# A fourth weight quarter split ahead of two combinations, with a query spill and small constants emitted later

## The chip, the cores and the metric

The kernel runs on one core of one Trainium2 chip. The metric is the device time of one launch in microseconds (us). Below, PE is the matrix engine (TensorE), DVE is VectorE, ACT is ScalarE, POOL is GpSimd and SP is SyncE, whose queue starts nearly all transfers (DMAs) here. Each engine has its own queue of instructions; they meet through semaphores. A time with two decimals such as 46.18 is a place in the profiled execution, counted from the start of its span.

## What is computed

One layer of a hybrid decoder runs on 1024 prompt tokens and 8 sample tokens that share the weights. First comes a large projection, then three branches (a gated linear recurrence, windowed attention, attention into 256 memory tokens), a gated merge, and a feed-forward block.

```python
z = x @ w_in
xr, yr, q, k, v, xq, g = jnp.split(z, SPLIT_IDX, axis=-1)
xc, conv_new = causal_conv(xr, conv_buf, conv_w, conv_b)
hs, h_new = rg_lru(xc, h0, lru_wa, lru_ba, lru_wx, lru_bx, lru_lambda)
a_out = hs * jax.nn.gelu(yr, approximate=True)
...
c_out = mem_attn(xq.reshape(B, T, N_XHEADS, XHEAD_DIM), mem_k, mem_v)
gates = jax.nn.sigmoid(g.reshape(B, T, N_BRANCH, D_MODEL) + b_gates)
merged = sum(gates[:, :, n] * (br @ w_branch[n]) for n, br in enumerate((a_out, s_out, c_out)))
h = layer_norm(ALPHA * x + merged @ w_out, ln1_g, ln1_b)
gt, up = jnp.split(h @ w_gate_up, 2, axis=-1)
h = layer_norm(ALPHA * h + (jax.nn.silu(gt) * up) @ w_down, ln2_g, ln2_b)
```

The change lies in the first 70 us or so, where `x @ w_in` begins.

## The kernel before

**Products of float32 numbers.** Every operand of a product is split into a high part (a cast on ACT, line 71) and a low part (a subtraction on DVE, line 72). A product is three matmuls: high by high, high by low, low by high. In the profile the parts of activations are `th` and `tl`, those of weights `u_0h` and `u_0l` and so on.

**The projection.** The output columns are cut into 30 units of two row tiles each (`UNITS`). The first unit, the first query tiles of the memory attention (`xq`), is done by `begin` with plain products while the activations come in by quarters `x`. From the second unit on the product of a 2 x 2 block matrix takes seven products of blocks in place of eight. For these, sums of weight quarters and of activation quarters are formed: `begin` makes the seven activation combinations `ts` once (`change` adds or subtracts quarters of `x` on DVE, line 204, and `keep` splits the result, for each of two halves `p` of the tokens), and `fast_quarter` makes a weight combination `i` of a unit: for `i` 1, 2, 4 and 5 an addition `us` on DVE (line 263), then the split. So `u_3l` is the low part of the weights of the fourth product (`i` = 3), whose weights are a plain quarter. `fast_step` runs product `i` of a unit for both halves, 12 matmuls each (lines 279 to 281, into `ub`, `uc` or `ud`), and copies or adds the result.

**The order.** `project` walks over `todo`, all pairs of unit and product, and asks for each weight combination three products ahead of its use. The first three of the second unit are asked for from within `begin`. A scheduler then orders each engine's instructions by its own plan, in which code that is written earlier is mostly preferred; after that each engine takes them strictly in that order.

**What stands around the change.** At the end of `begin`, `finish.done` takes the first unit's result (`za`, `zb`): for `xq` it copies the sample tokens' queries to `qdc`, and `spill` scales and splits both tiles (`hi_xq` on ACT, line 368; `za` and `zb` in place on DVE, line 369) and writes them to DRAM, to be read by the memory attention long after. It also queues the job `dec_mem`: the sample tokens' queries are turned (`drt`, line 770), copied (`drow_c`, line 771), written to DRAM and loaded again to all partitions (`dcq`, lines 772 and 783), then multiplied with cached keys (`dck`) on DVE, `dcj`, line 789. `lru_consts` computes constants of the recurrence and of the gates, mostly on 8 columns: some 26 DVE instructions and one on ACT (lines 657 to 677). `pump`, called after each product, emits a piece of the queued jobs.

Of the kernel before, what the change touches and what calls it, by code (L numbers as in the profile page):

```python
# [53 lines left out]
class Builder:  # L54
# [100 lines left out]
    def begin(self, rows, finish, load_next, next_quarter):  # L155


        nc, io, h = self.nc, self.io, D // 2
        pair = lambda name: tuple(self.tp.tile([P, 4, QS], F32R, tag="t", name=f"t{e}{name}", bufs=28) for e in "hl")
        x, hl, ts, w, ps = {}, {}, [[None] * 7, [None] * 7], [[None] * 2, [None] * 2], {}  # L160
        cols = lambda th, p: slice(HT * th + QN * p, HT * th + QN * (p + 1))

        def weight(j, e):
            raw = self.half_raw(io["win"][rows[j]][:, e * h:(e + 1) * h], h, f"ur0_{j}{e}")
            if e == 0:
                w[j] = [None, None, pair(f"w{j}")]
            flat = [a.rearrange("p k n -> p (k n)")[:, e * h:(e + 1) * h] for a in w[j][2]]
            w[j][e] = flat
            return lambda: self.split(*flat, raw)

        def keep(name, src, sign=1.0):
            tiles = pair(name)
            hi, lo = (a[:, :, :QN] for a in tiles)
            src = src.rearrange("p (k n) -> p k n", k=4)
            if sign < 0:
                self.split_scaled(hi, lo, src, sign)
            else:
                self.split(hi, lo, src)
            return tiles

        def fetch(kh, th, p):
            x[kh, th, p] = self.x_quarter(kh, th, p)

        def block(kh, th, p):
            hl[kh, th, p] = keep(f"{kh}{th}{p}", x[kh, th, p])

        def quarter(th, p, z):
            tags = ("mm", "t")
            for kh in range(2):
                xh, xl = (a[:, :, :QN] for a in hl[kh, th, p])  # L190
                for j in range(2):
                    if kh == 0:
                        ps[j] = self.bank(tags[j], f"u0{th}{p}{j}")[:, :QN]
                    wh, wl = w[j][kh]
                    for k in range(4):
                        c, first, last = slice(k * P, (k + 1) * P), kh + k == 0, kh == 1 and k == 3
                        nc.tensor.matmul(ps[j], wh[:, c], xh[:, k, :], start=first, stop=False)
                        nc.tensor.matmul(ps[j], wh[:, c], xl[:, k, :], start=False, stop=False)
                        self.last_mm = nc.tensor.matmul(ps[j], wl[:, c], xh[:, k, :], start=False, stop=last).ins
            for j in range(2):  # L200
                nc.scalar.copy(z[j][:, cols(th, p)], ps[j])

        def change(op, p, to, a, b):
            nc.vector.tensor_tensor(x[(*to, p)], x[(*a, p)], x[(*b, p)], op)
            return x[(*to, p)]

        s00 = weight(0, 0)
        fetch(0, 0, 0)
        s10, s01 = weight(1, 0), weight(0, 1)
        fetch(1, 0, 0)  # L210
        s11 = weight(1, 1)
        for th, p in ((0, 1), (1, 0), (1, 1)):
            fetch(0, th, p)
            fetch(1, th, p)
        z = self.zt("za0"), self.zt("zb0")
        s00()
        block(0, 0, 0)
        s10()
        s01()
        block(1, 0, 0)  # L220
        s11()
        quarter(0, 0, z)
        for th, p in ((0, 1), (1, 0), (1, 1)):
            block(0, th, p)
            block(1, th, p)
            quarter(th, p, z)
            if (th, p) == (1, 0):
                load_next()
                next_quarter(0)
        for p in range(2):  # L230
            ts[p][0], ts[p][3], ts[p][5] = hl[0, 0, p], hl[1, 0, p], hl[1, 1, p]
            change(ALU.subtract, p, (1, 1), (1, 1), (0, 1))
            ts[p][1] = keep(f"1_{p}", change(ALU.subtract, p, (0, 1), (0, 0), (0, 1)))
        next_quarter(1)
        for p in range(2):
            ts[p][2] = keep(f"2_{p}", change(ALU.add, p, (0, 0), (1, 1), (0, 0)), -1.0)
        next_quarter(2)
        finish.done(*z)
        for p in range(2):
            ts[p][4] = keep(f"4_{p}", x[1, 1, p])  # L240
        for p in range(2):
            ts[p][6] = keep(f"6_{p}", change(ALU.subtract, p, (1, 0), (0, 0), (1, 0)))
        return ts

    def fast_load(self, u, src0, src1):
        h = D // 2
# [76 lines left out]
    def project(self):  # L323

        nc, io, tc = self.nc, self.io, self.tc
        self.qdc = self.cst.tile([P, KT * NB], F32, name="qdc")
        self.qds = self.cst.tile([P, KT * NB], F32, name="qds")
        self.kd = self.cst.tile([P, 2 * NB], F32, name="kd")
        self.vd = self.cst.tile([NB, 256], F32, name="vd")
        self.lru_setup()  # L330
        self.side, self.pumped = (deque(), deque()), 0
        n = len(UNITS)
        finish = [Finish(self, kind, j) for kind, j in UNITS]
        st = {}

        def load(u):
            a, b = finish[u].rows
            st[u] = self.fast_load(u, io["win"][a], io["win"][b])
            st[u]["load"]((0, 0), (0, 1), (1, 0), (1, 1))

        ts = self.begin(finish[0].rows, finish[0], lambda: load(1), lambda i: self.fast_quarter(st[1], i))
        with tc.issue_after(self.x_loaded):
            self.load_consts()
            self.load_lru()
        self.lru_consts()
        todo = [(u, i) for u in range(1, n) for i in range(7)]
        ahead = 3
        for k, (u, i) in enumerate(todo):
            if i == 1 and u + 1 < n:
                load(u + 1)  # L350
            if k + ahead < len(todo):
                v, j = todo[k + ahead]
                self.fast_quarter(st[v], j)
            self.fast_step(st[u], i, ts, finish[u])
            self.pump()
            if i == 6:
                del st[u]
        while any(self.side):
            self.pump()
        nc.sync.dma_start(self.scr["c"][:, :, TP:T], self.cdec)  # L360
        self.store_lru()
# [950 lines left out]
```

## Time and profile before

| | |
|---|---|
| median of 3 runs | 2013.3 us (2012.09 to 2013.93) |
| the profiled execution's own time | 2013.24 us |
| its span | 2011.5 us |
| PE's mean granted clock | 0.994 |
| PE idle before its first matmul | 6.0 us |
| PE's longest later waits | 4.6 (`bra`, line 105), 4.1 (`uc`, line 281) us |
| the projection's products end near | 658 us |

How the profile is read: the span runs from the first to the last instruction. In a timeline a row gives the start, the duration, engine, line, operation, `out<-in` by the program's names, shapes and a count; a bracket gives how long the engine stood idle before it and what released it. In a table of stretches a row gives the stretch, its length, then for PE, PE's weight loads, DVE, ACT and POOL the busy time with the number of instructions, then PE's granted clock, the DMA engines' share and GB/s. In the list of waits a row gives who waited for whom, the sum in us, how often, and the longest. A group of the page gives the count, the busy time, the mean ns of one, and the idle time ahead.

### The profile page before, as it was taken

Reading aid. Unit: us, or ns where it says so; the run is one execution under the profiler, and the core shown is the slowest. Engines: PE = TensorE matmul, PEld = TensorE weight load, DVE = VectorE, ACT = ScalarE, POOL = GpSimd, SP = SyncE. Lnnn points to the kernel's source line nnn. Section 1 sums busy time; section 2 is a strip of 40 time slices with the busy share of each in tenths; the row PEclk is TensorE's granted clock in tenths of the full one; section 3 lists DMA queues with packets and bytes.
Section 4 is the critical chain, followed back from the end, with each engine's and each line's share of the span. In section 5 each row is a group of like instructions: output and inputs, shape, how many; then the busy total and the mean of one; then the engine's idle time right before and its main releaser. Section 6 shows DMA issues by size and latency. Waiting matters only on the chain.

```text
span 2011.5 us, 35413 instructions
## 1 busy us (share of the span) xinstructions
PE 1962.2 (98%) x13756; PEld 1929.8 (96%) x13756; DVE 1197.3 (60%) x2558; ACT 878.9 (44%) x1921; POOL 112.4 (6%) x160
## 2 busy tenths in 40 slices
PE   7999999999999999999999999999999999999997
PEld 7999999999999899989999999999999999999996
DVE  8789778878665555498876658423222332232457
ACT  6556555546564555398763334322111221122324
POOL 0001000000000000021110002100000000000001
PEclk9999999999999999999999999999999999999999
DMA  5454454563233865667435320111111111111102
GB/s 220 151 174 171 165 190 137 176 197 125 76 142 107 294 217 188 160 187 218 121 87 167 124 87 22 63 63 58 48 43 42 53 49 47 53 43 43 57 28 85
DMA packets 140441, 235.44 MB, mean 117 GB/s; under 512 B 17280, under 2 KB 69584, under 8 KB 140240
## 3 DMA queue, kind: packets, MB, share of 16 engines
q1 hardware_dynamic: 140272, 233.17, 35.8%
q8 instruction: 108, 1.77, 0.4%
q14 instruction: 61, 0.50, 0.1%
HBM read 179.95 MB, written 55.23 MB: 117 GB/s over the span
## 4 chain that ended last, share of the span: by engine, by line
PE 70%; ACT 4%; DVE 3%; DMA 3%; issue 1%; SPq 0%; ACTq 0%; POOL 0%; DVEq 0%; POOLq 0%
PE fg L107 4%; PE fg L105 4%; PE fg L106 4%; PE fu L107 4%; PE fu L105 4%; PE fu L106 4%; PE d L105 3%; PE d L107 3%; PE d L106 3%; PE ub L279 2%; PE ub L281 2%; PE ub L280 2%; PE brs L105 2%; PE brs L106 2%; PE brs L107 1%; PE bra L106 1%
## 5 line engine op out<-in xcount | busy, mean ns | idle before, releaser
L105 PE MATMUL fg<-hH,wfg_h 128*128 128x384 f32 (+1 forms) x528 | 169.2, 320 | 5.9 <-ACT wfg_h L71 3.0
L106 PE MATMUL fg<-hL,wfg_h 128*128 128x384 f32 (+1 forms) x528 | 168.4, 319 | 0.4 <-DVE hL L1053 0.4
L107 PE MATMUL fg<-hH,wfg_l 128*128 128x384 f32 (+1 forms) x528 | 168.3, 319 | 0.2
L107 PE MATMUL fu<-hH,wfu_l 128*128 128x384 f32 (+1 forms) x528 | 167.7, 318 | 0.0
L106 PE MATMUL fu<-hL,wfu_h 128*128 128x384 f32 (+1 forms) x528 | 167.6, 317 | 0.0
L105 PE MATMUL fu<-hH,wfu_h 128*128 128x384 f32 (+1 forms) x528 | 167.6, 318 | 0.0
L1071 DVE TENSOR_TENSOR ft<-ft,fu 128x384 f32<-128x384 f32 (+1 forms) x66 | 33.8, 513 | 141.4 <-PE fu L107 141.3
L1069 DVE SCALAR_TENSOR_TENSOR ft<-ft,fg 128x384 f32<-128x384 f32 (+1 forms) x66 | 33.8, 512 | 139.6 <-ACT ft L1068 137.6
L105 PE MATMUL d<-gH,wd_h 128*128 128x384 f32 (+1 forms) x360 | 114.4, 318 | 0.0
L106 PE MATMUL d<-gL,wd_h 128*128 128x384 f32 (+1 forms) x360 | 114.2, 317 | 0.0
L107 PE MATMUL d<-gH,wd_l 128*128 128x384 f32 (+1 forms) x360 | 114.2, 317 | 0.0
L71 ACT CAST gH<-ft 128x384 fp32r<-128x384 f32 (+1 forms) x66 | 31.7, 480 | 183.2 <-DVE ft L1071 183.1
L105 PEld LDWEIGHTS fg<-hH,wfg_h 128*128 128x128 f32 x528 | 99.6, 189 | 7.3 <-ACT wfg_h L71 3.4
L106 PEld LDWEIGHTS fg<-hL,wfg_h 128*128 128x128 f32 x528 | 99.8, 189 | 1.0 <-DVE hL L1053 0.9
L107 PEld LDWEIGHTS fg<-hH,wfg_l 128*128 128x128 f32 x528 | 99.8, 189 | 0.9 <-DVE wfg_l L72 0.9
L107 PEld LDWEIGHTS fu<-hH,wfu_l 128*128 128x128 f32 x528 | 99.2, 188 | 0.0
L105 PEld LDWEIGHTS fu<-hH,wfu_h 128*128 128x128 f32 x528 | 99.2, 188 | 0.0
L106 PEld LDWEIGHTS fu<-hL,wfu_h 128*128 128x128 f32 x528 | 99.2, 188 | 0.0
L1068 ACT ACTIVATE ft<-fg 128x384 f32<-128x384 f32 (+1 forms) x66 | 30.1, 456 | 139.8 <-PE fg L107 139.8
L1095 DVE SCALAR_TENSOR_TENSOR acc<-d,acc 128x384 f32<-128x384 f32 (+1 forms) x48 | 24.8, 516 | 108.4 <-PE d L107 108.4
L565 ACT ACTIVATE bp<-bp,bst 128x257 f32<-128x257 f32 (+1 forms) x128 | 62.8, 493 | 18.1 <-DVE bst L561 18.0
L281 PE MATMUL uc<-th,u_3l 128*128 128x258 f32 x232 | 66.4, 287 | 4.1 <-DVE u_3l L72 4.1
(960 smaller groups left out, 6857.3 us busy)
## 6 DMA issues: line engine op xcount, KB each, us to landing
ur<-win SPq DMA_DIRECT2D x120, 256.0 KB, 2.9
dck<-cmk SPq DMA_DIRECT2D x32, 256.0 KB, 2.9
dcv<-cmvT SPq DMA_DIRECT2D x32, 256.0 KB, 3.5
st<-scr_q SPq DMA_DIRECT2D x32, 256.0 KB, 5.2
scr_g<-za SPq DMA_DIRECT2D x12, 516.0 KB, 3.3
scr_g<-zb SPq DMA_DIRECT2D x12, 516.0 KB, 4.0
x<-xQ SPq DMA_DIRECT2D x8, 516.0 KB, 8.0
scr_a<-ge SPq DMA_DIRECT2D x8, 516.0 KB, 3.0
```

The lines of the kernel that those rows point to most:

```text
L71: ins = self.nc.scalar.copy(hi, src).ins
L105: nc.tensor.matmul(ps, sh, mh, start=i == 0, stop=False)
L106: nc.tensor.matmul(ps, sh, ml, start=False, stop=False)
L107: self.last_mm = nc.tensor.matmul(ps, sl, mh, start=False, stop=closes and i == last).ins
L279: mm(sh[:, w], xh, start=opens and k == 0, stop=False)
L280: mm(sh[:, w], xl, start=False, stop=False)
L281: self.last_mm = mm(sl[:, w], xh, start=False, stop=k == 3).ins
L565: nc.scalar.activation(x, x, AF.Exp, bias=st[:, g:g + 1], scale=-1.0, accum_out=st[:, 4 + g:5 + g])
L1068: nc.scalar.activation(t, pg, AF.Tanh, scale=0.5)
L1069: nc.vector.scalar_tensor_tensor(t, t, 1.0, pg, op0=ALU.add, op1=ALU.mult)
L1071: nc.vector.tensor_mul(t, t, pu)
L1095: nc.vector.scalar_tensor_tensor(a, ps, 0.5, a, op0=ALU.mult, op1=ALU.add)
```

## The change

```diff
@@ begin
         next_quarter(2)
-        finish.done(*z)
+        next_quarter(3)
         for p in range(2):
             ts[p][4] = keep(f"4_{p}", x[1, 1, p])
         for p in range(2):
             ts[p][6] = keep(f"6_{p}", change(ALU.subtract, p, (1, 0), (0, 0), (1, 0)))
-        return ts
+        return ts, z
@@ project
-        ts = self.begin(finish[0].rows, finish[0], lambda: load(1), lambda i: self.fast_quarter(st[1], i))
+        ts, z0 = self.begin(finish[0].rows, finish[0], lambda: load(1), lambda i: self.fast_quarter(st[1], i))
...
-        self.lru_consts()
...
-            if k + ahead < len(todo):
+            if 0 < k < len(todo) - ahead:
                 v, j = todo[k + ahead]
                 self.fast_quarter(st[v], j)
             self.fast_step(st[u], i, ts, finish[u])
+            if k == 2:
+                finish[0].done(*z0)
+            if k == 4:
+                self.lru_consts()
             self.pump()
```

The fourth weight quarter of the second unit is now asked for in `begin`, ahead of the activation combinations of the fifth and seventh products (`ts` 4 and 6); the loop skips it at its first step. The spill of the first unit and its `dec_mem` job come after the third product of the second unit, the constants after its fifth. No instruction is added or removed. Below the changed lines the line numbers are three higher.

On DVE, the place around the old spill, as a piece of the difference (names carry buffer numbers; a line with - is before, with + the change, without either both):

```order
 L78 SCALAR_TENSOR_TENSOR tl_1_425<-x_126,th_1_424 128x4x258
-L369 SCALAR_TENSOR_TENSOR za_138<-za_138,hi_xq_435 128x1024
+L72 TENSOR_TENSOR tl_0_439<-x_132,th_0_438 128x4x258
 L72 TENSOR_TENSOR u_2l<-us_2_428,u_2h 128x512
-L369 SCALAR_TENSOR_TENSOR zb_139<-zb_139,hi_xq_441 128x1024
-L72 TENSOR_TENSOR tl_0_447<-x_132,th_0_446 128x4x258
-L72 TENSOR_TENSOR tl_1_451<-x_136,th_1_450 128x4x258
+L72 TENSOR_TENSOR u_3l<-ur_01_330,u_3h 128x512
+L72 TENSOR_TENSOR tl_1_443<-x_136,th_1_442 128x4x258
 L204 TENSOR_TENSOR x_122<-x_114,x_122 128x1032
 L204 TENSOR_TENSOR x_128<-x_126,x_128 128x1032
```

`u_3l` has moved up to the row behind `u_2l`; before, it stood behind both spill rows, four `tl`, the two L204 and the first constants.

Also on DVE, in the change, the rows from the second unit's last split to the first rows of the third unit (`u2_0l` is the third unit's first low part; `dcq0` the loaded queries, `za1`, `zb1` the second unit's results):

```order
L72 TENSOR_TENSOR u1_6l_597<-ur1_11_334,u1_6h_596 128x512
L792 SCALAR_TENSOR_TENSOR dcj0_0_0_592,dcs0_587<-dck0_0_590,dcq0_0_588 128x256
L306 TENSOR_TENSOR za1_600<-uc1_0_601,p1s1_0_473 128x258
L792 SCALAR_TENSOR_TENSOR dcj0_0_1_594,dcs0_587<-dck0_0_590,dcq0_0_588 128x256
L306 TENSOR_TENSOR za1_600<-uc1_1_615,p1s1_1_488 128x258
L72 TENSOR_TENSOR u2_0l_630<-ur2_00_490,u2_0h_629 128x512
L308 SCALAR_TENSOR_TENSOR zb1_633<-ub1_0_460,p5s1_0_517 128x258
```

Before, the first `dcj` rows stood ahead of the fifth, sixth and seventh low parts of the second unit, among the constants; now they stand behind the last of these and ahead of `u2_0l`.

On SP, the queue of transfers around the spill and the queries, before:

```order
L370 DMA scr_xq<-hi_xq_435 128x1024
L370 DMA scr_xq<-hi_xq_441 128x1024
L371 DMA scr_xq<-za_138 128x1024
L371 DMA scr_xq<-zb_139 128x1024
L772 DMA dcq_538<-drow_c_539 8x256
L783 DMA dcq_0_546<-dcq_538 128x512
```

and in the change:

```order
L373 DMA scr_xq<-hi_xq_569 128x1024
L373 DMA scr_xq<-hi_xq_575 128x1024
L82 DMA ur_10_494<-win 128x512
L82 DMA ur_11_496<-win 128x512
L775 DMA dcq_580<-drow_c_581 8x256
L82 DMA ur_00_816<-win 128x512
L786 DMA dcq_0_588<-dcq_580 128x512
L374 DMA scr_xq<-za_138 128x1024
L374 DMA scr_xq<-zb_139 128x1024
```

Weight loads `ur` of the third and fourth units have moved ahead of the queries' write and load, and the two `z` tiles of the spill go out behind them.

On ACT the casts of `ts` 4 and of `u_3h` stand where `hi_xq` of the second tile stood; that `hi_xq` follows three result copies later, and `drow_c` stands behind the cast of `u_4h`. On PE the two `drt` transposes stand ahead of the fourth product in place of the second, and six matmuls of the third unit's first product stand ahead of the second unit's seventh.

## The prediction

> **What bounds the kernel now.** The page comes first, then the waits of TensorE (PE) in it.
>
> ```profile
> span 2011.5 us, 35413 instructions
> PE 1962.2 (98%) x13756; PEld 1929.8 (96%) x13756; DVE 1197.3 (60%) x2558; ACT 878.9 (44%) x1921; POOL 112.4 (6%) x160
> L281 PE MATMUL uc<-th,u_3l 128*128 128x258 f32 x232 | 66.4, 287 | 4.1 <-DVE u_3l L72 4.1
> ```
>
> PE is busy 98% of the span, so only an idle piece of PE, or a stretch at a lower clock, can give time back. The third row holds such a piece: the product with the fourth weight quarter once waited 4.1 us for `u_3l`. The timeline of PE shows it, in the second unit:
>
> ```profile
> 41.44 0.28 PE L279 MATMUL uc<-th,u_3h 128*128 128x258 f32 x1
> 41.68 0.28 PE L279 MATMUL uc<-th,u_3h 128*128 128x258 f32 x1
> 46.18 0.39 PE L281 MATMUL uc<-th,u_3l 128*128 128x258 f32 x1 [4.11 <-DVE u_3l L72]
> 50.19 0.29 PE L279 MATMUL ub<-th,u_4h 128*128 128x258 f32 x1
> 53.08 0.28 PE L279 MATMUL ud<-th,u_5h 128*128 128x258 f32 x1
> ```
>
> Four matmuls of the product run, then PE stands 4.11 us. Matmuls from 50.19 to 53.08 are one product of 24, 2.89 us, or 0.120 each. The 20 from 46.18 to 50.19 took 4.01 where 20 x 0.120 is 2.41. The table of stretches says why, and what VectorE (DVE) does meanwhile:
>
> ```profile
> 32.50:46.00 13.50, 9.58 (x80) 9.33 (x79) 13.40 (x18) 9.90 (x19) 0.00 (x0) 1.00 0.51 197
> 46.18:49.81 3.63, 3.63 (x18) 3.63 (x18) 3.63 (x16) 1.95 (x4) 0.00 (x0) 0.53 0.37 131
> 58.00:72.00 14.00, 14.00 (x118) 14.00 (x117) 14.00 (x33) 7.50 (x18) 0.00 (x0) 1.00 0.47 160
> ```
>
> After the wait the granted clock is 0.53. So this place costs 4.11 us of waiting and 4.01 - 2.41 = 1.60 us of slow clock, **5.71 us** together. But DVE is busy without a break before it (13.40 of 13.50) and long after it (14.00 of 14.00). The delay of PE is also what lets DVE catch up.
>
> **The fourth quarter.** DVE before, in its timeline:
>
> ```profile
> 34.00 1.22 DVE L78 SCALAR_TENSOR_TENSOR tl<-x,th 128x1032 fp32r<-128x1032 f32 x1
> 35.14 1.21 DVE L369 SCALAR_TENSOR_TENSOR za<-za,hi_xq 128x1024 fp32r<-128x1024 f32 x1
> 36.28 0.68 DVE L72 TENSOR_TENSOR u_2l<-us,u_2h 128x512 fp32r<-128x512 f32 x1
> 36.88 1.21 DVE L369 SCALAR_TENSOR_TENSOR zb<-zb,hi_xq 128x1024 fp32r<-128x1024 f32 x1
> 40.48 2.37 DVE L204 TENSOR_TENSOR x<-x,x 128x1032 f32<-128x1032 f32 x2
> 42.77 0.17 DVE L657 TENSOR_SCALAR nsnk<-vec 128x16 f32<-128x16 f32 x1
> 45.44 0.69 DVE L72 TENSOR_TENSOR u_3l<-ur,u_3h 128x512 fp32r<-128x512 f32 x1
> 46.19 0.42 DVE L789 SCALAR_TENSOR_TENSOR dcj<-dck,dcq 128x256 f32<-128x256 f32 x1
> 46.53 0.20 DVE L665 RECIPROCAL lruc<-lruc 128x8 f32<-128x8 f32 x1
> ```
>
> From start to start: a row over about 1032 columns holds DVE 1.14 us (34.00 to 35.14), one over 512 columns 0.60 (36.28 to 36.88), one over 256 columns 0.34 (46.19 to 46.53). ACT's part, and the queries' rows on SyncE (SP):
>
> ```profile
> 34.26 1.05 ACT L368 ACTIVATE hi_xq<-zb 128x1024 fp32r<-128x1024 f32 x1
> 37.72 0.36 ACT L771 COPY drow_c<-drt_c 8x256 f32<-8x256 f32 x1
> 40.20 0.38 ACT L304 COPY u2s<-ub 128x258 f32<-128x258 f32 x1 [0.63 <-PE ub L281]
> 38.53 0.34 SPq L772 DMA_DIRECT2D dcq<-drow_c  x1
> 41.29 0.82 SPq L783 DMA_DIRECT2D dcq<-dcq  x2
> dcq<-dcq SPq DMA_DIRECT2D x4, 256.0 KB, 3.4
> ```
>
> In the new order of DVE (first piece shown with the change) the first `tl` of the fifth product takes the place of the spill at 35.14. Its cast takes the place of `hi_xq` on ACT, 34.26 to 35.31, so DVE starts it at 35.35 instead. Then 1.14 for it and 0.60 for `u_2l`: `u_3l` starts at 37.09 and ends at 37.78. PE asks for it at 41.68. The wait of 4.11 goes with 3.9 us to spare, and with it the slow clock: **-5.71 us**.
>
> **What is late next: the fifth quarter.** Behind `u_3l` on DVE come five long rows (`tl`, two L204, two `tl`) and one sum: 37.69 + 5 x 1.14 + 0.60 = 43.99, so `u_4l` ends at 44.68. Product four starts at 41.44 + 2.89 = 44.33, and its third matmul wants `u_4l` at 44.57. That is a wait of about **0.15 us**; it is nothing if DVE runs 0.2 early, and up to 1 if a cast on ACT behind the copy at 40.20 holds a `tl` up.
>
> **What is late after that: the head of DVE's queue.** The second and third pieces of the order matter most. Before, the first `dcj` (memory scores of the sample group) stood at 46.19, with its queries long asked for: the load went out at 41.29. Now the spill is emitted after product two, the row copy `drow_c` stands on ACT behind the cast of `u_4h`, and everything behind `dcj` on DVE waits with it.
> - DVE is free for `dcj` after `us_5` 0.60, `za` 1.14, `u_5l` 0.60, `zb` 1.14, `u_6l` 0.60, counted from 43.99 + 0.60: 44.59 + 4.08 = 48.67.
> - The copy: ACT takes `u2s` at 41.4, `th` 0.95, `u_4h` 0.52, `drow_c` 0.36, so it ends at 43.5. The write of the row goes out then; before, the load followed its write after 2.76 us (38.53 to 41.29), so the load goes at 46.3. The median landing is 3.4 us: 49.7. One `ur` load ahead of it in SP's queue waits for `us_5`, done at 45.3, which is earlier.
> - So `dcj` starts at 49.7, not 48.67. Behind it stand `za`, `dcj`, `za` and then `u_0l` of the third unit: 49.7 + 4 x 0.34 = 51.06, and it ends at 51.75.
> - PE: product four with its wait, then product five: 44.33 + 0.15 + 2 x 2.89 = 50.26. Its order now puts six matmuls of the third unit's first product there; two use `u_0h`, the third wants `u_0l` at 50.50. **A new wait of 51.8 - 50.5 = 1.3 us.**
>
> Bounds of this term, which no row of before has in this order: a landing by 48.6 leaves 0.3 us (DVE alone is then late), a landing at the 8.0 us of the first loads gives 5.9. I take 1.3, from the row of the same transfer.
>
> **The constants.** They add nothing, their some 26 small rows only move, from before to behind the new wait. There the first gate matrix row is the point to watch, since DVE has no slack.
>
> ```profile
> 66.26 0.51 DVE L72 TENSOR_TENSOR xcl<-xc,xch 128x344 fp32r<-128x344 f32 x1
> 72.62 0.43 DVE L789 SCALAR_TENSOR_TENSOR dcj<-dck,dcq 128x256 f32<-128x256 f32 x1 [0.20 <-DMA dck<-cmk]
> ```
>
> From the first `dcj` to `xcl` DVE took 66.26 - 46.19 = 20.07 us, with no idle until 72.62. In the new order three splits and two sums of the second unit stand ahead of it (-5 x 0.60), two `dcj` fewer (-0.7), seven small rows more (+0.5), one split of the third unit more (+0.6): 17.5. So `xcl` starts at 49.7 + 17.5 = 67.2 and ends at 67.7. PE has 130 matmuls from `u_0l` to it, 51.8 + 15.7 = 67.5. A wait of **0.2 us**, between nothing and 1. Later DVE has idle time before its rows again, so I let nothing more be lost; the spill's writes are used some 600 us later.
>
> **The sum.** -5.71 + 0.15 + 1.3 + 0.2 = **-4.1 us**. The profiled execution took 2013.24 us (span 2011.5 and 1.74 around it), and the median of the three runs is 2013.3, so the two sums agree: **2009.2 us**.
>
> **A rule on the clock.** What does the new wait do to the clock? Rows of PE after idle pieces of the same size:
>
> ```profile
> 424.15 0.27 PE L380 MATMUL vt<-ident,za 128*8 128x128 f32 x1 [1.72 <-DVE v L392]
> 1312.40 0.44 PE L105 MATMUL fg<-hH,wfg_h 128*128 128x384 f32 x1 [1.49 <-ACT wfg_h L71]
> 1359.50 0.44 PE L105 MATMUL fg<-hH,wfg_h 128*128 128x384 f32 x1 [1.48 <-ACT wfg_h L71]
> 1360.77 0.53 PE L106 MATMUL fg<-hL,wfg_h 128*128 128x384 f32 x1
> ```
>
> Pieces of 1.72 and 1.49 us were followed by full speed, one of 1.48 by matmuls of 0.53 us from 1360.77 on. So a wait of 1.3 probably costs no clock, yet can. [...]
>
> **Rivals.**
> - *No new wait at `u_0l`.* The query load lands before DVE asks. For: the transfer is small and the queue was empty in this stretch of before. Against: the write and the load follow each other, 2.76 + 3.4. Then -5.71 + 0.15 + 0.3 = -5.3: 2008.0.
> - *The new wait halves the clock.* As at 1359.50, with the 1.60 us of the old place: -4.1 + 1.6 = -2.5: 2010.8.
> - *Later waits of the projection change.* The order of DVE and SP shifts for the whole phase, and PE has these there:
>
> ```profile
> PE vt L380 <- DVE v L392: 2.4, 2, 1.7
> PE ub L279 <- ACT zb L1182: 1.0, 2, 0.8
> PE ub L279 <- ACT p1s L304: 0.9, 1, 0.9
> PE ub L279 <- ACT zb L1184: 0.8, 1, 0.8
> PE ub L279 <- DVE zb L308: 0.5, 1, 0.5
> ```
>
>   They sum to 5.6 us. Halved, the time is 2009.2 - 2.8 = 2006.4; grown by half, 2012.0. Nothing in the rows says which.
> - *Slower: the queries hold DVE as long as the constants did.* The mechanism is the one at `dcj`, with a load that queues behind weights as the first loads did:
>
> ```profile
> x<-xQ SPq DMA_DIRECT2D x8, 516.0 KB, 8.0
> ```
>
>   Landing at 46.3 + 8.0 = 54.3 makes the wait 5.9 and, being over 4.11, costs the 1.60 of clock too: -5.71 + 0.15 + 5.9 + 1.6 = +1.9, 2015.2. It is slower from a landing at 52.4 on, and by over 0.2% from 56.4 on. Against: DMA was at 0.51 here.
>
> **How the numbers follow.** Forecast 0.52, no new wait 0.17, halved clock 0.13, later waits 0.14 (0.06 less, 0.08 more), queries late 0.04. A measurement of this kernel tells about 0.2%, 4.0 us, from no change, and the forecast of -4.1 lies on that edge: it gives half to faster, half to same. Faster: 0.26 + 0.16 + 0.01 + 0.06 = 0.49. Slower by over 0.2%: 0.04, from queries late and from later waits that grow more than I price. Same: 0.47. The range takes in the bounds of the new wait from 0.3 to 3 and most of the shifts: 2006.9 to 2012.3.
>
> **What would show it.** No idle on PE before `u_3l`, and granted clock 1.0 through 50 us. `u_3l` on DVE near 37.1. DVE idle about 1 us before the first `dcj`, ended by the load of the queries. PE waiting about 1.3 us for `u_0l` near 51.8. At full clock and equal later waits, the start of the third unit's second product is about 4.3 us earlier than before. The forecast is wrong if that start has moved less than 3 or more than 5 us, or if the later waits sum to something far from 5.6.

## The result and the profile after

| | before | after |
|---|---|---|
| median | 2013.62 us (2011.81 to 2017.14, 6 runs) | 2005.74 us (2003.19 to 2008.32, 6 runs) |
| ratio | | 0.9957, 95% interval 0.9943 to 0.9970 |
| profiled execution's own time | 2013.24 us | 2003.19 us |
| its span | 2011.5 us | 2001.3 us |
| start of the first `bra`, behind the projection | 662.4 us | 655.1 us |

The change made the kernel 7.9 us faster in the medians, where 4.1 were forecast, and the time lies below the range. The first rows of the page of the kernel after:

```profile
span 2001.3 us, 35401 instructions
PE 1959.4 (98%) x13756; PEld 1927.1 (96%) x13756; DVE 1195.0 (60%) x2558; ACT 878.8 (44%) x1921; POOL 115.3 (6%) x160
```

The number of instructions on PE, DVE and ACT is the same; the 12 fewer of the total are not among these engines' counts. First the place that the prediction worked out, in the timeline of PE after the change (start, duration, engine, line, operation; a bracket holds the idle time ahead and what ended it):

```profile
41.24 0.36 PE L279 MATMUL uc<-th,u_3h 128*128 128x258 f32 x1
44.22 0.28 PE L279 MATMUL ub<-th,u_4h 128*128 128x258 f32 x1
47.39 0.28 PE L279 MATMUL ud<-th,u_5h 128*128 128x258 f32 x1
50.26 0.28 PE L279 MATMUL ub<-th,u_0h 128*128 128x258 f32 x1
52.02 0.39 PE L281 MATMUL ub<-th,u_0l 128*128 128x258 f32 x1 [1.37 <-DVE u_0l L72]
57.66 0.28 PE L279 MATMUL ud<-th,u_1h 128*128 128x258 f32 x1
```

Product four runs from 41.24 to 44.22 without a stop, products four and five follow each other, and the new wait stands at `u_0l` of the third unit: 1.37 us. The last row is the first matmul of the third unit's second product. The same row of before:

```profile
61.72 0.28 PE L279 MATMUL ud<-th,u_1h 128*128 128x258 f32 x1
```

So PE is 61.72 - 57.66 = 4.06 us earlier there. DVE and the queue of SP after the change, for the same place:

```profile
36.97 0.68 DVE L72 TENSOR_TENSOR u_3l<-ur,u_3h 128x512 fp32r<-128x512 f32 x1
43.89 0.69 DVE L72 TENSOR_TENSOR u_4l<-us,u_4h 128x512 fp32r<-128x512 f32 x1
47.97 0.69 DVE L72 TENSOR_TENSOR u_6l<-ur,u_6h 128x512 fp32r<-128x512 f32 x1
49.92 0.42 DVE L792 SCALAR_TENSOR_TENSOR dcj<-dck,dcq 128x256 f32<-128x256 f32 x1 [1.26 <-DMA dcq<-dcq]
51.28 0.68 DVE L72 TENSOR_TENSOR u_0l<-ur,u_0h 128x512 fp32r<-128x512 f32 x1
```

```profile
43.43 0.35 SPq L775 DMA_DIRECT2D dcq<-drow_c  x1
46.03 0.33 SPq L786 DMA_DIRECT2D dcq<-dcq  x1
```

The write of the queries went out at 43.43 and their load at 46.03; DVE stood 1.26 us at the first `dcj` until it had landed, with `u_0l` behind it. The table of stretches has the clock where it was 0.53 before (stretch, length, busy time of PE, its weight loads, DVE, ACT and POOL, granted clock, DMA share, GB/s):

```profile
46.18:49.81 3.63, 3.63 (x33) 3.63 (x32) 2.47 (x4) 0.70 (x2) 0.00 (x0) 1.00 0.90 286
```

The granted clock is 1.00, and 33 matmuls start where 18 did. Up to here the forecast holds. What it had not is in the list of PE's waits from 62 to 650 us (who waited for whom; sum in us, times, longest), after the change:

```profile
PE ub L279 <- ACT zb L1187: 1.2, 1, 1.2
PE g L106 <- DVE xcl L72: 0.5, 1, 0.5
```

Two rows, 1.7 us together. The five rows of before, shown with the prediction, sum to 5.6. The two waits for `vt`, 2.4 us, are gone, and so is the one for `p1s`, 0.9. PE was 3.75 us ahead of before at 72 us (read from equal matmuls of the two timelines), and 7.35 at the first `bra`. So half of the gain up to there arises between 72 us and the end of the projection, in waits that no changed line names. The prediction named later waits far from 5.6 us as a sign of being wrong, and that sign came.

### The profile page after: what moved, and what is told of

Read it like the earlier page. It is cut to its first block, busy times and chain, and to the rows that moved or that the text cites. A ratio compares the mean times of both kernels' runs of the same rounds, so it can differ in the third digit from the quotient of the medians.

```text
span 2001.3 us, 35401 instructions
## 1 busy us (share of the span) xinstructions
PE 1959.4 (98%) x13756; PEld 1927.1 (96%) x13756; DVE 1195.0 (60%) x2558; ACT 878.8 (44%) x1921; POOL 115.3 (6%) x160
## 4 chain that ended last, share of the span: by engine, by line
PE 87%; DVE 5%; ACT 4%; DMA 3%; issue 1%; SPq 0%; ACTq 0%; POOL 0%; DVEq 0%; POOLq 0%
PE ub L279 5%; PE ub L281 5%; PE ub L280 5%; PE fg L107 4%; PE fg L105 4%; PE fg L106 4%; PE fu L107 4%; PE fu L105 4%; PE fu L106 4%; PE d L105 3%; PE d L107 3%; PE d L106 3%; PE ud L281 2%; PE ud L280 2%; PE ud L279 2%; PE brs L105 2%
## 5 line engine op out<-in xcount | busy, mean ns | idle before, releaser
L106 PEld LDWEIGHTS d<-gL,wd_h 128*128 128x128 f32 x360 | 67.7, 188 | 0.0
```

The costliest lines, as they stand in the source:

```text
L106: nc.tensor.matmul(ps, sh, ml, start=False, stop=False)
```

## Experiments

**Theory:** the change does two things. Locally it removes the wait for `u_3l` (4.11 us) with its slow clock (0.53), and adds one at `u_0l`. And it starts the first sample-query job `dec_mem` behind the third product of the second unit in place of the first. `pump` emits a step of these jobs at every second product and the four jobs follow each other without a gap, so each of their steps, up to the last near 440 us, stands two products later against the projection. Some of the waits after 62 us arise from where the jobs' DVE rows meet the projection's. **Rivals:** the later waits come from the late start of PE, or from chance; or the weight quarter that was moved brings the gain.

In the tables, "later waits" is the sum of the list of PE's waits from 62 to 650 us, and "of these vt, u_2h" the part between 380 and 430 us. The ratio is that to before, run on the same chip in the same session; kernels of different sessions are compared by it, not by their times. The list counts waits alone, no stretches of slow clock.

### How far the numbers repeat

The two kernels again, unchanged.

> The kernel before, once more with a profile. In the first profile PE's waits in the projection behind 60 us sum to 5.5 us (0.8 at 125, 0.2 at 210, 0.5 at 269, 0.8 at 275, 0.9 at 389, 0.6 and 1.7 at 416 and 424). Theory 'job place' (where the sample-query job stands relative to the units decides them): the same places wait again, sum 4.5 to 6.5 us. Theory 'head start' (PE being 4 us earlier decides them): the same. Theory 'chance' (transfers' timing from run to run decides them): other places, sum anywhere from 2 to 8 us. All: the wait for u_3l is again 4.1 +- 0.2.

> The changed kernel, once more with a profile and timed beside the others of this call. In the first profile the later waits of the projection sum to 1.8 us (1.2 at 121, 0.5 at 278, 0.1 at 416). 'Job place' and 'head start': again 1.3 to 2.5 us at these places. 'Chance': 2 to 8 us. All: the wait for u_0l near 52 us is 1.0 to 1.7 us. Ratio to before 0.994 to 0.997.

> The changed kernel again, for the comparison with the two beside it: 0.995 to 0.997 of before, idle pieces of TensorE 8.0 to 8.7 us up to 62 us, waits from 62 us to the first bra 1.5 to 2.2 us at 121 to 122 us and one other place, none for vt.

> The changed kernel once more, beside the one with the queries ahead: 0.995 to 0.997 of before; a wait of 1.3 to 1.9 us for u_0l at 52 to 53 us; later waits 1.5 to 2.6 us.

| kernel | time, us | ratio (95%) | wait at the start | later waits | of these vt, u_2h |
|---|---|---|---|---|---|
| before, first profile | 2013.62 | | `u_3l` 4.11 | 5.6 | 3.3 |
| before, again | 2018.02 (one run) | | `u_3l` 4.09 | 6.2 | 3.8 |
| after, first | 2005.74 | 0.9957 (0.9943 to 0.9970) | `u_0l` 1.37 | 1.7 | 0 |
| after, again | 2007.15 | 0.9968 (0.9957 to 0.9978) | `u_0l` 1.85 | 2.1 | 0 |
| after, third | 2007.17 | 0.9962 (0.9948 to 0.9975) | `u_0l` 1.65 | 2.5 | 0.5 |
| after, fourth | 2005.45 | 0.9958 (0.9946 to 0.9970) | `u_0l` 1.62 | 2.2 | 0.4 |

The wait at the start repeats. Of the later ones, six of the seven of before come back within 3 us of their place; after the change only the one at 121 to 123 us stands in all four traces, and the others vary (222, 278, 330, 416 or 418 us), where the same places were expected. But the sums are 3.1 to 4.5 us shorter after the change in each pairing of the traces, so their fall is not chance. Single runs of before spread over some 10 us (2009.2 to 2019.4 over all sessions), which is why waits of 1 us are read from traces here, not from times.

### Which part of the change does it

`quarter_only` moves the quarter alone:

```diff
@@ begin
         next_quarter(2)
+        next_quarter(3)
         finish.done(*z)
@@ project
-            if k + ahead < len(todo):
+            if 0 < k < len(todo) - ahead:
```

> Kernel before with one part of the change: the fourth weight quarter is split directly behind the third; the query spill and the recurrence constants stay where they were. Theory (the wait of the second unit is a sum of DVE rows, and the later waits go with the place of the sample-query job): the wait for u_3l goes, but the spill and the constants now stand ahead of u_4l, wanted about 2.8 us later, so 1.3 us or less of the 4.1 is won up to 62 us (idle pieces of TensorE 10 to 11 us up to there, after the change 8.0 to 8.7); the job starts in the place of before, so the waits from 62 us to the first bra stay at 4.5 to 6.2 us; time within 2 us of before. Rival (moving the quarter is what brings the gain, and the later waits fall because the weights are ahead): idle pieces up to 62 us about 8 us, later waits about 2 us, time as after the change (0.9968 of before).

`late_only` moves the spill with its job and the constants, and leaves the quarter:

```diff
@@ begin
         next_quarter(2)
-        finish.done(*z)
...
-        return ts
+        return ts, z
@@ project
-        self.lru_consts()
...
             self.fast_step(st[u], i, ts, finish[u])
+            if k == 2:
+                finish[0].done(*z0)
+            if k == 4:
+                self.lru_consts()
```

> The other part alone: query spill behind the third product of the second unit, constants behind its fifth, and the fourth quarter asked for in the loop as before. Theory: with 5.9 us of DVE rows gone from ahead of it u_3l still ends by 41.2 us, wanted at 41.7, so TensorE does not wait for it, idle pieces up to 62 us 8.0 to 8.8 us as after the whole change; the sample-query job starts two products later as after the whole change, so later waits 1.8 to 2.6 us; time as after the whole change, within 1.5 us. Rival (the quarter has to move): a wait of 1 to 4 us for u_3l stays at 42 us, with the halved clock behind it, time within 2 us of before.

The quarter alone: 2015.14 us, ratio 1.0007 (0.9998 to 1.0016). The rest alone: 2006.52 us, ratio 0.9962 (0.9952 to 0.9972), level with the whole change. DVE and the list of PE's waits from 20 to 650 us with the quarter alone:

```profile
35.82 0.69 DVE L72 TENSOR_TENSOR u_3l<-ur,u_3h 128x512 fp32r<-128x512 f32 x1
47.09 0.69 DVE L72 TENSOR_TENSOR u_4l<-us,u_4h 128x512 fp32r<-128x512 f32 x1
```

```profile
PE ub L280 <- ACT u_4h L71: 3.6, 1, 3.6
PE vt L381 <- DVE v L393: 2.4, 2, 1.6
PE ub L280 <- ACT zb L1183: 1.2, 2, 0.8
PE ub L280 <- ACT zb L1185: 0.8, 1, 0.8
```

`u_3l` is there long before PE comes to it near 42 us, but the spill and the constants still stand ahead of the next sum and `u_4l`, so a wait of 3.6 us comes one product later, again with a granted clock of 0.5 behind it (from 47.65, for 3.4 us), and the later waits for `vt` are those of before. With the rest alone, DVE:

```profile
41.16 0.69 DVE L72 TENSOR_TENSOR u_3l<-ur,u_3h 128x512 fp32r<-128x512 f32 x1
50.04 0.43 DVE L791 SCALAR_TENSOR_TENSOR dcj<-dck,dcq 128x256 f32<-128x256 f32 x1 [0.62 <-DMA dcq<-dcq]
```

`u_3l` comes just in time in its old place among the combinations, PE does not wait for it, and the later waits sum to 1.5 us. The quarter that the change moves is worth nothing by itself: on this stretch of DVE, busy without a break, the row moved forward passed its wait on to the next one; only the rows moved behind the stretch shortened it.

`spill_late` is the whole change but for the constants, which stand in their old place again:

```diff
@@ project, from the changed kernel
+        self.lru_consts()
         todo = [(u, i) for u in range(1, n) for i in range(7)]
...
-            if k == 4:
-                self.lru_consts()
```

> The changed kernel with the recurrence constants back in their old place (quarter moved, spill and first job late). Theory: DVE has the constants' 2.1 us ahead of u_4l again, so TensorE waits 0.5 to 1.5 us for it at 44 to 46 us; the wait for u_0l falls by as much as TensorE is later (it goes by the landing of dcq at 50 us), so up to 62 us it is level with the changed kernel within 0.7 us; job's place as after the change, later waits 1.5 to 2.6 us; 0.996 to 0.997 of before. Rival (late constants matter later on, where the recurrence's units begin): later waits of 3 us or more.

2009.13 us, ratio 0.9973 (0.9964 to 0.9983), 2.0 to 3.7 us above the four medians of the whole change, which are of other sessions and whose intervals overlap with this one. PE waits 0.8 us for `u_4h`, as expected. But the wait for `u_0l` did not shrink; it grew to 2.2 us. DVE shows it:

```profile
51.47 0.42 DVE L791 SCALAR_TENSOR_TENSOR dcj<-dck,dcq 128x256 f32<-128x256 f32 x1 [1.78 <-DMA dcq<-dcq]
51.90 0.69 DVE L72 TENSOR_TENSOR u_6l<-ur,u_6h 128x512 fp32r<-128x512 f32 x1
53.81 0.68 DVE L72 TENSOR_TENSOR u_0l<-ur,u_0h 128x512 fp32r<-128x512 f32 x1
```

The queries' load landed 1.5 us later than in the first profile after, and `u_6l` and some small rows of the constants now stand between the first `dcj` and `u_0l`. So the expectation that this wait goes by a landing at 50 us was wrong; why the load landed later is open. The later waits, 3.1 us, lie over the expected 2.6.

### The job's place

`job_late` is before with the first job alone queued two products later; `job_early` is the changed kernel with the job's copies of the queries and its queueing back in `begin`, so that it starts in its old place:

```diff
@@ project, from before (job_late)
             self.fast_step(st[u], i, ts, finish[u])
+            if k == 2:
+                self.side[1].append(self.dec_mem(0))
@@ done
-            if self.kind == "xq":
+            if self.kind == "xq" and j:
                 b.side[1].append(b.dec_mem(j))
```

```diff
@@ begin, from the changed kernel (job_early)
         next_quarter(3)
+        for e in range(2):
+            nc.scalar.mul(self.qdc[:, e * NB:(e + 1) * NB], z[e][:, TP:T], 1.0 / 16.0)
+        self.side[1].append(self.dec_mem(0))
@@ done: neither for the first unit
```

> The kernel before, with one edit: the first sample-query job is queued two products later, as the changed kernel has it; spill, quarter and constants stay. 'Job place': the wait for u_3l stays at 4.1 us with its slow clock, the later waits of the projection fall from 5.5 to about 2 us (those before the v transposes near 416 and 424 go), time 3 to 4 us below before (ratio 0.998 to 0.9985). 'Head start' and 'chance': later waits stay at 5 to 6 us or anywhere, time within 1 us of before (ratio 0.9995 to 1.0005 for 'head start').

> The changed kernel, with one edit: the two copies of the sample queries and the job that uses them are queued in the first unit again, where before had them; the spill stays late. 'Job place': no wait for the queries' load, the wait for u_0l falls from 1.4 to 0.3 to 0.8 us (DVE alone), but the waits near the v transposes come back, later waits 4.5 to 5.5 us, so the time is 2 to 3 us above the changed kernel. 'Head start': later waits stay near 2 us, the time is 0.5 to 1 us below the changed kernel.

`job_4later` and `job_6later` are the changed kernel with the first job queued at `k == 3` and `k == 5`, so that its first step stands two and four products later still:

```diff
@@ project, from the changed kernel (job_4later; job_6later: k == 5)
+            if k == 3:
+                self.side[1].append(self.dec_mem(0))
             if k == 4:
                 self.lru_consts()
@@ done
-            if self.kind == "xq":
+            if self.kind == "xq" and j:
                 b.side[1].append(b.dec_mem(j))
```

> The changed kernel with the first sample-query job queued two products later still (first step behind the fifth product of the second unit instead of the third; spill and constants as changed). Theory: the new wait of 1.37 us for u_0l of the third unit is there because the first dcj stands in DVE's order ahead of it and waits for the queries' load; with the job 5 us later the load has landed, and the wait falls to 0.4 us or less. The later waits go with the job's place against the products: not the pattern of before (vt waits of 0.5 to 2.2 us near 416 and 424, ub waits near 125 and 210); sum from 62 us to the first bra 1 to 4 us. Time 0 to 2 us below the changed kernel. Rival (the later waits have nothing to do with the job): the same pieces as after the change, 1.8 to 2.1 us, at the same places (121 and 278 us).

> The same with the job queued four products later than in the changed kernel (first step behind the seventh product of the second unit). Theory: no wait for u_0l either (0.4 us or less); the later pattern is again another one, since the job's steps meet other products, sum 1 to 6 us. Rival (job has no part in it): pieces as after the change, 1.8 to 2.1 us at 121 and 278 us.

| kernel | job's first step behind product | time, us | ratio (95%) | later waits | of these vt, u_2h |
|---|---|---|---|---|---|
| before | 1 | 2013.62 | | 5.6 | 3.3 |
| quarter_only | 1 | 2015.14 | 1.0007 (0.9998 to 1.0016) | 4.4 | 2.4 |
| job_early | 1 | 2010.43 | 0.9980 (0.9970 to 0.9990) | 4.5 | 2.0 |
| job_late | 3 | 2012.23 | 0.9991 (0.9980 to 1.0002) | 4.2 | 0 |
| late_only | 3 | 2006.52 | 0.9962 (0.9952 to 0.9972) | 1.5 | 0.2 |
| spill_late | 3 | 2009.13 | 0.9973 (0.9964 to 0.9983) | 3.1 | 0 |
| job_4later | 5 | 2009.96 | 0.9983 (0.9972 to 0.9994) | 6.4 | 0.2 |
| job_6later | 7 | 2005.99 | 0.9961 (0.9946 to 0.9977) | 3.7 | 1.4 |

In these kernels, wherever the job starts behind the first product, the waits near 416 and 424 us stand in the trace, 1.7 to 3.2 us for `vt`; wherever it starts behind the third, they are gone or half a microsecond. Putting it back (`job_early`) costs the changed kernel 3.3 us in the medians of one session. But the place is not the only thing that counts. `job_late` missed its expectation: it lost the `vt` waits and got 2.1 us of waits for `xcl`, a row of the recurrence, at 226 and 284 us, so that 4.2 us of later waits stayed where about 2 were expected, and its time cannot be told from that of before (the interval takes in 1). With the job later still the wait for `u_0l` is gone, as expected, but `job_4later` has the worst sum of all, against its expectation of 0 to 2 us below the changed kernel. Its largest piece, in the timelines of PE, ACT and DVE:

```profile
232.13 0.58 PE L279 MATMUL ub<-th,u_0h 128*128 128x258 f32 x1 [3.25 <-ACT zb L1189]
```

```profile
230.65 0.21 ACT L1208 ACTIVATE qdc<-za 128x8 f32<-128x8 f32 x1 [3.62 <-DVE za L311]
231.72 0.37 ACT L1189 ACTIVATE zb<-ub 128x258 f32<-128x258 f32 x1
```

```profile
228.91 0.43 DVE L818 SCALAR_TENSOR_TENSOR dcw<-dcv,dcpb 128x256 f32<-128x256 f32 x1 [1.72 <-DMA dcv<-cmvT]
230.20 0.42 DVE L311 TENSOR_TENSOR za<-ud,u2s 128x258 f32<-128x258 f32 x1
```

DVE stands 1.72 us at a row of the job (`dcw`) whose cached values (`dcv`) have not landed; behind it stand two more such rows and then a `za` that ACT needs; ACT in turn stands with the copy that frees PE's `ub` behind it. So here a side job's late load reached PE through two engines, 1.72 us at DVE's row and 3.62 at ACT's copy; at most 1.72 of the 3.25 us are the load's, the rest lies in the rows between. A stretch of slow clock follows, which the list of waits does not count:

```profile
232.13:237.75 5.62, 5.62 (x26) 5.62 (x27) 5.58 (x8) 4.67 (x8) 0.00 (x0) 0.50 0.89 345
```

At 0.120 each the 26 matmuls would take 3.1 us, so this costs some 2.5 us more.

### One job alone, and none

`last_job_later` is before with an empty first step in the last of the four jobs alone:

```diff
@@ dec_mem, from before
+        if h == 3:
+            yield
         nc, io, ph = self.nc, self.io, self.dp
```

> Kernel before, with only the last of the four sample-query jobs set one step (two products) later by an empty first step. Theory (the two vt waits near 416 and 424 us come from the value part of the last job, whose dcw stand on DVE ahead of the rows of v that free vt's banks): both vt waits go (2.4 to 3.2 us in before), the wait for u_3l at 46 to 47 us and the waits at 125, 210 and 276 us stay; the wait at 389 us for u_2h may change too; time 1 to 3 us below before. Rival (vt waits come from elsewhere, such as the lateness of TensorE against VectorE that the missing 4 us at the start bring): vt waits of 1.5 to 3 us stay, time within 1 us of before.

2010.37 us, ratio 0.9979 (0.9970 to 0.9989): one empty step takes 3.7 us from the kernel before in the medians of the session; the list of waits explains 2.3 to 2.9 of it (5.6 and 6.2 in two traces of before, 3.3 here), and in one of the two traces of before a slow stretch of 3.4 us follows the last `vt` wait (at 427.31), which the list does not count. That list, PE's waits from 62 to 650 us:

```profile
PE ub L279 <- ACT zb L1184: 1.4, 2, 0.8
PE ub L279 <- ACT zb L1186: 1.0, 1, 1.0
PE ub L279 <- DVE zb L308: 0.7, 2, 0.5
PE vt L380 <- DVE v L392: 0.2, 1, 0.2
```

The waits that belong to the first three jobs' time stay (at 125, 211, 270 and 276 us), those for `vt` fall from 2.4 to 0.2, and that for `p1s` is gone. DVE in before shows how they arose (`dcw` are the rows of the job's value part, `v` those that free the banks which `vt` writes):

```profile
413.11 0.43 DVE L813 SCALAR_TENSOR_TENSOR dcw<-dcv,dcpb 128x256 f32<-128x256 f32 x1 [2.35 <-DMA dcpb<-dcpd]
415.35 0.42 DVE L392 TENSOR_TENSOR v<-vt,v 128x256 fp32r<-128x256 f32 x1
421.57 0.43 DVE L813 SCALAR_TENSOR_TENSOR dcw<-dcv,dcpb 128x256 f32<-128x256 f32 x1 [2.18 <-DMA dcv<-cmvT]
423.67 0.42 DVE L392 TENSOR_TENSOR v<-vt,v 128x256 fp32r<-128x256 f32 x1
```

and after the change:

```profile
408.07 0.42 DVE L395 TENSOR_TENSOR v<-vt,v 128x256 fp32r<-128x256 f32 x1
411.15 0.42 DVE L395 TENSOR_TENSOR v<-vt,v 128x256 fp32r<-128x256 f32 x1
414.02 0.43 DVE L816 SCALAR_TENSOR_TENSOR dcw<-dcv,dcpb 128x256 f32<-128x256 f32 x1 [1.73 <-DMA dcpb<-dcpd]
416.00 0.42 DVE L395 TENSOR_TENSOR v<-vt,v 128x256 fp32r<-128x256 f32 x1
```

DVE stands at the first `dcw` in both, 2.35 and 1.73 us. Before, the `v` row that PE waits for until 415.82 is behind it; after the change the rows at 408.07 and 411.15 are through by then, and the next is ready before PE asks.

To part the local gain from the jobs', both kernels were run without the four jobs:

```diff
@@ done, from before and from the changed kernel
-            if self.kind == "xq":
-                b.side[1].append(b.dec_mem(j))
@@ build
         self.cdec = self.cst.tile([P, KT, NB], F32, name="cdec")
+        self.nc.gpsimd.memset(self.cdec, 0.0)
```

> Kernel before without the four sample-query jobs (their part of the output stays zero). Theory (the local gain of some 4 to 5.7 us and the later gain by the jobs' place are two things): the wait of 4.1 us for u_3l and the halved clock stay; all waits for vt, and those at 210, 270, 276 and 389 us, go; the waits from 62 us to the first bra sum to 1.5 us or less. Rival (the later waits of before come from the late start of the projection): they stay at 3 us or more without the jobs.

> The changed kernel without the four jobs (their part of the output stays zero). Theory: no first dcj stands ahead of u_0l, so that wait of 1.4 to 1.9 us is gone; idle pieces up to 62 us 6.5 to 7.2 us, later waits as in the kernel before without jobs, within 0.7 us of it; so the two kernels without jobs differ by 5.0 to 6.2 us, which is the 4.1 us wait, the 1.6 us of halved clock and nothing later, and not by the 7 to 8 us that the whole kernels differ by. Rival (the later gain doesn't need the jobs): they differ by 8 to 9.5 us.

Medians 2002.95 and 1996.54 us, 6.4 apart (ratios to before 0.9953, interval 0.9939 to 0.9967, and 0.9912, interval 0.9898 to 0.9926). The only row of PE's waits from 20 to 650 us in before without jobs:

```profile
PE uc L281 <- DVE u_3l L72: 4.3, 1, 4.3
```

After the change without jobs there is none but the one ahead of `bra`. The first `bra` stands at 653.54 and 647.53, 6.0 apart. Of this 5.5 arise in the projection: the wait of 4.3 and the slow clock of 1.6, less some 0.4 that the changed kernel loses at the start and at `u_4l`. The other 0.5 is the wait ahead of `bra` itself, 5.81 and 5.30. So all later waits of PE in the projection need the jobs, in both kernels, and without them the earlier start of the projection changes nothing later.

Where in the projection the later gain lies can be read from equal matmuls: the first one of the 17th unit's second product and the first one of the 19th unit's seventh, with the three waits of the last job's time (389, 416 and 424 us) between them. Before:

```profile
363.12 0.28 PE L279 MATMUL ud<-th,u_1h 128*128 128x258 f32 x1
424.29 0.37 PE L279 MATMUL ub<-th,u_6h 128*128 128x258 f32 x1
```

and after the change:

```profile
359.13 0.28 PE L279 MATMUL ud<-th,u_1h 128*128 128x258 f32 x1
416.61 0.36 PE L279 MATMUL ub<-th,u_6h 128*128 128x258 f32 x1
```

| kernel | from the third unit's second product (61.72 in before) to the first of the two, us | between the two, us |
|---|---|---|
| before, two traces | 301.4, 301.9 | 61.2, 61.7 |
| quarter_only | 300.9 | 60.4 |
| job_early | 302.3 | 59.9 |
| after, four traces | 301.0 to 301.9 | 57.2 to 57.8 |
| late_only | 300.7 | 57.5 |
| last_job_later | 302.7 | 57.5 |
| job_late | 303.9 | 57.3 |
| both without jobs | 296.6 | 56.7 |

The first 300 us are the same before and after the change, though the waits there differ. The later gain, 3.4 to 4.5 us, lies in the second stretch alone, where the last job's value part runs, and the empty step in that job has the same 3.7 of it as the first profile after. `job_late` has it too, and loses 2.0 to 2.5 us ahead of it.

### The new wait

`queries_ahead` and `queries_again` are one kernel: the changed one, with the copies, transposes and the write of the first job's queries back in `begin`, and an extra step between them and the first `dcj`, so that the job's DVE work keeps its new place:

```diff
@@ begin, from the changed kernel
         next_quarter(3)
+        for e in range(2):
+            nc.scalar.mul(self.qdc[:, e * NB:(e + 1) * NB], z[e][:, TP:T], 1.0 / 16.0)
+        self.side[1].append(self.dec_mem(0))
@@ dec_mem
         self.dec_rows(self.qdc, 2 * h, qr, "c")
+        if h == 0:
+            yield
@@ done: neither for the first unit
```

> The changed kernel, with the copy of the sample queries, their transposes and their write taken out of the late query part and done where begin ends; the first job's first dcj stays behind the third product of the second unit. Theory: dcq lands before DVE comes to the first dcj, so the wait of 1.4 to 1.9 us for u_0l of the third unit goes (0.3 us or less) and the later waits stay as after the change, 1.5 to 2.2 us; time 1.1 to 1.8 us below the changed kernel (0.9991 to 0.9994 of it). Rival (the copies on ScalarE and the transposes on TensorE push u_4h and u_4l later, or the later waits come back because the job's DMAs run earlier): 0.3 to 1 us at 44 to 46 us and later waits of 4 to 6 us, time 1 to 3 us above the changed kernel.

> The kernel with the queries ahead, again. If the wait for u_0l that it takes away is worth its length, it stays 1 to 2.5 us below the changed kernel; if the 1.5 us come back as later waits for xcl, as the one trace of it has them (1.6 us in two), the two are within 1 us.

2004.80 and 2003.95 us, ratios 0.9947 (0.9935 to 0.9959) and 0.9955 (0.9942 to 0.9967); the changed kernel beside it took 2007.17 and 2005.45. DVE in the second:

```profile
48.41 0.42 DVE L797 SCALAR_TENSOR_TENSOR dcj<-dck,dcq 128x256 f32<-128x256 f32 x1
50.37 0.68 DVE L72 TENSOR_TENSOR u_0l<-ur,u_0h 128x512 fp32r<-128x512 f32 x1
```

No wait for the load, none of PE for `u_0l`. The later waits were 4.0 us in the first trace and 1.3 in the second, against 2.5 and 2.2 in the changed kernel beside it. So in the medians the gain is 1.5 to 2.4 us, about the length of the wait, but the intervals overlap, and the first trace, with 1.6 us of waits for `xcl`, missed the expected 1.5 to 2.2 us of later waits: what the wait is worth is not shown closely. Its medians are the lowest here of a kernel that computes everything.

## Why the prediction was right here and wrong there

- **The fourth quarter, -5.71 us: right in sum, wrong in what earns it.** `u_3l` started at 36.97 (37.09 predicted), the wait and the slow clock went. Without the jobs 5.5 us arise in the projection, that term and little else. But the prediction put it under the quarter's new place and did not part it from the spill and the constants that leave the stretch; `late_only` has the gain without the new place, and `quarter_only` hasn't it. The rows that left the stretch earn it.
- **The fifth quarter, 0.15: right.** `u_4l` started at 43.89 and ended at 44.58, where 44.68 was predicted. PE lost 0.28 us there: two matmuls of 0.12 each took from 44.34 to 44.86.
- **The head of DVE's queue, 1.3 us: right.** `dcj` at 49.92 (49.7), released by the queries' load, and 1.37 us of PE at 52.02 (1.3 near 51.8). The write at 43.43 and the load at 46.03 stand where the working had them (43.5 and 46.3). The wait varied from 1.37 to 1.85 in four traces. The clock stayed at 1.00 behind it in all four, so the rival of the halved clock didn't come.
- **The constants, 0.2 at `xcl`: too small to tell.** `xcl` started at 67.42 (67.2), and PE lost some 0.3 us between the third unit's second product (4.06 ahead) and 72 us (3.75 ahead). That the constants leave their old place has no term of its own in the prediction; with them there (`spill_late`) the medians are 2.0 to 3.7 us higher, across sessions.
- **The rest of the projection: the step that failed.** It reads "Later DVE has idle time before its rows again, so I let nothing more be lost", and as a rival it priced a halving of the later waits at -2.8 us, with the words "Nothing in the rows says which". They fell by 3.9 us, from 5.6 to 1.7. DVE's idle time was no cover: part of it is DVE standing at a row of the job whose data have not landed, with rows behind it that PE needs. The rows of before said this at 413.11 and 421.57, behind the two waits for `vt`, the largest row of the list, and `pump` said that each job step moves by two products. These were a reason to give the later waits a term of their own instead of none: the stretch from 363 to 424 us became 3.4 to 4.5 us shorter. Which waits a new place brings in their stead no row of before shows, as `job_4later` makes plain.
- **The sum.** With the later term at its measured size, 4.1 + 3.1 to 3.9 (5.6 less 1.7 to 2.5 in the four traces) is 7.2 to 8.0 us; the four differences of medians are 7.9, 7.3, 6.9 and 8.6. The profiled pair differs by 10.1; of the 2.7 us that arise behind `bra`, 1.6 is the slow clock at 1360.77 of before, which one trace of the changed kernel has and its first profile has not (below).

What stays open: why the waits other than `vt` and `p1s` come and go. They add nothing to the change's own gain (the table of the two stretches), but they cost `job_late` more than half of its. With the job behind the third product, `job_late`, `spill_late` and one trace of the kernel with the queries ahead have 3.1 to 4.2 us of later waits, about half of it for `xcl`, and six other traces 1.3 to 2.5. The jobs are needed for them, but whether they go by the landing of single loads or by the exact start of PE was not tried.

## What to carry to other kernels

When a change moves the start of a side job that is emitted in steps beside the main work, all its later steps move with it: look in the trace for places where an engine stands at a row of that job with rows of the main work behind it, and see in the new order which rows come out ahead. A new place can also bring new waits, as `job_4later` did (6.4 us). On an engine that is busy without a break, look what the row behind the moved one will wait for: here moving the waited-for row forward passed the wait on (4.11 us for `u_3l` became 3.6 for `u_4h`), and taking work out of the stretch removed it. Running both kernels without the side job parts the two effects at once.

## What was unexpected in the hardware

The clock after short waits. The feed-forward part has two waits of 1.48 us, some 47 us apart (at 1312.40 and 1359.50 in before), in every one of the 18 traces. After 13 of these 36 the granted clock fell to 0.5 for 3.4 us, after 23 it did not. Two rows of tables of stretches, each from 0.77 us behind the end of the second wait, of the changed kernel run again and of its first profile:

```profile
1355.30:1358.80 3.50, 3.50 (x11) 3.50 (x12) 1.71 (x3) 1.27 (x3) 0.00 (x0) 0.51 0.59 198
```

```profile
1351.51:1355.01 3.50, 3.50 (x20) 3.50 (x21) 1.71 (x3) 1.27 (x3) 0.00 (x0) 1.00 0.63 187
```

The same place of the program: 11 matmuls start in one and 20 in the other. Such a fall cost some 1.6 us: the stretch from the first `fg` to the first `d` took 185.8 us in the first profile after, with none, and 187.4 in before, with one. Two of them would make 3.2 us, an estimate from these numbers, and so much of a run's time can differ between executions of one kernel.

The length of a wait alone did not decide: in before no fall came behind 1.49 us at 1312.40, and one behind 1.48 at 1359.50. In before the falls start at 46.43, 660.83 and 1360.56; the distances, 614.40 and 699.73 us, are 180 and 205 times 3.413 us, the length of the first and the last of these falls. The step of this length ahead of the fall at 1360.56, and the step of the fall:

```profile
1357.15:1360.56 3.41, 1.82 (x12) 1.29 (x11) 1.94 (x4) 2.04 (x5) 0.00 (x0) 1.00 0.00 0
1360.56:1363.97 3.41, 3.41 (x12) 3.41 (x11) 1.42 (x3) 0.98 (x2) 0.00 (x0) 0.50 0.67 243
```

PE was idle for 1.59 us of the first, the wait and a short stop behind it. In steps of the same length, counted from the falls of each trace, the three other such waits of before and of the first profile after, with no fall behind them, have at most 1.48, 1.46 and 0.82 us of idle time in one step. But the step from 421.90 to 425.31 of before has 1.71 us of it, and behind it the clock stayed at 1.00. So what decides is not shown.
